# Hybrid stream block on one core: SiLU on ScalarE, two norms from row-major input, decay matrices built together, key products 14 steps later, FFN input sums right after the third norm

## Chip, cores, metric

One Trainium2 chip, one core. The metric is the device time of one launch in microseconds; before the change its median over 3 runs is 1247.88 us (1247.12 to 1248.3).

In this text PE is TensorE, DVE is VectorE, ACT is ScalarE, POOL is GpSimd and SP is SyncE. PSUM is the memory that TensorE writes.

## What is computed

One layer on 512 tokens of width 1024 (float32), batch 1:

```
h  = rmsnorm(x)
qa,ka,va,za,alpha,beta,qb,kb,vb,ga,gb = split(h @ w_in)
q,k,v = silu(causal_conv4(qa,ka,va))
oa = rmsnorm(gated_deltanet(q,k,v,alpha,beta)) * silu(za)      # 8 heads of 128
ob = band attention(qb,kb,vb) with a relative bias               # 16 heads of 64
x  = x + (sigmoid(ga)*(oa@w_a_out) + sigmoid(gb)*(ob@w_b_out)) @ w_o
x  = x + cross attention(rmsnorm(x), rmsnorm(mem))                # 4 heads, 256 memory rows
x  = x + (silu(gate)*up) @ w_down,  gate,up = rmsnorm(x) @ w_gate_up   # 2816 wide
out = rmsnorm(x)
```

In the gated DeltaNet, each head takes, per chunk of 128 tokens here, the matrix `exp(G_i - G_j)` for i >= j (the decay matrix, from cumulated sums G of the log decays), multiplies it into `k k^T` and into `q k^T`, and solves a unit triangular system with the first product.

## The kernel before, in words

Activations lie with features on the 128 partitions and the 512 tokens along the free dimension: x is eight tiles of 128x512. Every product is made in three matmuls from high and low halves (`split`, L113 to L119: ACT makes the high half, DVE or POOL the low half by a subtraction). `weights` (L121) loads a weight block of 128x8x128 (512 KB) on SP's queue and splits it; raw, high and low tiles have three buffers each. A block of eight k steps (`block_steps`, L131) issues three matmuls per step, so 24 per block.

PE's order is the order of the program text; on the other engines and on the DMA queues the framework's scheduler places instructions by a simulated timeline. Side work runs in generators: `drive` (L176) issues one step of the main products and then advances every generator in `pending` by one `yield`; `wait(n)` passes n steps. So the numbers in `wait` set how far behind the main products a dependent PE operation is put. A second generator, `side`, is advanced at a given rate after a given delay.

The stages that matter here, in order:

- **Start.** For k = 0 to 7, x's tile k is loaded, scaled and split, and the products of the first 272 columns (z0: the decay and beta columns and the first two heads' z) are added up in four PSUM banks (L236). `square_sum` (L200) squares each tile on ACT and adds it on POOL (L206). This loop fixes the order of ACT and DVE by hand.
- **First norm** (`first_norm`, L264), beside the z1 products: `rms_cols` (L208) sums the squares over partitions with matmuls against ones and gets the reciprocal root as a column per token tile (the power runs on POOL, L217); `z_evac` (L284) empties the z banks with this scale and makes SiLU from Tanh; `rms_rows` (L220) turns the columns into a row tile `rrow`; POOL multiplies x by it (L276), and the result is split into h. z0, z1 and the keys of heads 0 and 1 use the unscaled x, everything later uses h.
- **Keys.** k0 to k7, with z and gate blocks between them (`go`, L691). `decay` (L306) computes the log decays on small tiles, waits 26 steps, takes the cumulated sums with matmuls (psG, L329), waits 4, transposes them (psT, L334) and writes them to DRAM (dG). `k_after` (L374) does a head's causal convolution (`conv`: one ACT pass, three DVE multiply-adds, Tanh on ACT at L354, one DVE operation at L355), waits 12 steps, multiplies k by itself (kk, L388), takes the norms from its diagonal, loads the head's row of G for all partitions (L399), adds a triangular mask on POOL (L401), exponentiates on ACT (L404), and writes the system's matrix L (L412); after every second head L's 32x32 blocks are stored to DRAM on SP (L423).
- **Values and inverse.** The v blocks (`v_after`, conv and, 12 steps later, the transposes vn at L519), the later gates and z groups, and the first queries. Beside them `inverse_blocks` (L526) gathers L's blocks, inverts them by 31 pairs of DVE operations (L538, L540), and builds up the full inverses with small matmuls from L576 on.
- **Queries, states, outputs, band attention, merge.** `memory` (L835) splits the memory rows' features and computes their norm like the first one.
- **Cross attention**, then **FFN**. The first three of the 22 gate/up column blocks are plain products (`ffn_gemm`, `ffn_after`), during which `ffn_sums` (L1084) builds the normed input in combined halves (fh, fl); the other 19 are done by `unit` (L1136), seven products of half size in place of eight. `gu_split` splits the finished FFN rows for the down projection; for the first five blocks this is done after unit 12.

The norms work with 2 * SiLU(u), that is `(tanh(u/2) + 1) * u`, where later norms divide the factor out; hence the 4s and 0.5 in L393, L416, L482, L519 and thereabouts.

Of the kernel before, what the change touches and what calls it, by code (L numbers as in the profile page):

```python
# [8 lines left out]
F32 = mybir.dt.float32  # L9
F32R = mybir.dt.float32r  # L10
AF = mybir.ActivationFunctionType
ALU = mybir.AluOpType
# [14 lines left out]
NEG = -1e30  # L27

# [11 lines left out]
def hybrid_block(  # L40
    ctx: ExitStack,
    tc: tile.TileContext,
    xT, memT, consts, wz0, wz, wq, wk, wv, wqb, wkb, wvb, wga, wgb,
# [47 lines left out]
    def PD(name):  # L91
# [10 lines left out]
                            pattern=[[1, P]], channel_multiplier=-1)  # L102
    mneg = cp.tile([P, P], F32, name="mneg")
    nc.gpsimd.memset(mneg, 0.0)
    nc.gpsimd.affine_select(out=mneg, in_=mneg, compare_op=ALU.is_ge, fill=NEG, base=0,
# [113 lines left out]

    def rms_rows(rs, ntok, name, dst):  # L220

        ps = PS(name)
        for tt in range(ntok):
            nc.tensor.matmul(out=ps[:, tt * P : (tt + 1) * P], lhsT=rs[:, tt : tt + 1].to_broadcast([P, P]),
                             rhs=ident, start=True, stop=True)
        nc.scalar.activation(dst, ps[:, : ntok * P], AF.Copy)
# [3 lines left out]
    acc1 = TMP("acc", "acc")  # L230
# [13 lines left out]
    with tc.manual_schedule(engines={mybir.EngineType.Activation, mybir.EngineType.DVE}):  # L244
        for k in range(KD):
# [11 lines left out]
            for j in range(max(0, k - 1), k if k < KD - 1 else KD):  # L257
                square_sum(acc1, xt[j], j)
# [5 lines left out]
    def first_norm():  # L264
        yield from wait(1)
        stat["cols"] = rms_cols(acc1, NT, "rstd")
# [7 lines left out]
        for k in range(KD):  # L274
            hi, lo = G("a", "hh", F32R), G("a", "hl", F32R)
            nc.gpsimd.tensor_tensor(out=xt[k], in0=xt[k], in1=rrow, op=ALU.mult)  # L276
            split(hi, lo, xt[k], gain(C_MIX, k))
            h.append((hi, lo))
            yield
# [4 lines left out]
    def z_evac(g):  # L284

        def f(tt, ps):
            o = 16 if g == 0 else 0
            r = stat["cols"][:, tt : tt + 1] if g <= 1 else 1.0
            if g == 0:
                nc.scalar.activation(ab[:, tt, :], ps[:, 0:16], AF.Copy, scale=r)  # L290
            zc, th = TMP("zc", "c")[:, :256], TMP("zt", "th")[:, :256]
            nc.scalar.activation(zc, ps[:, o : o + 256], AF.Copy, scale=r)
            nc.scalar.activation(th, zc, AF.Tanh, scale=0.5)
# [12 lines left out]
    def decay():  # L306
        nc.scalar.activation(beta, ab[:, :, AH:], AF.Exp, scale=-1.0)
        nc.vector.tensor_scalar_add(out=beta, in0=beta, scalar1=1.0)
        nc.vector.reciprocal(out=beta, in_=beta)
        nc.vector.tensor_tensor(out=sp_, in0=ab[:, :, :AH], in1=hrow(C_DT), op=ALU.add)  # L310
        nc.scalar.activation(u_, sp_, AF.Abs)
        nc.scalar.activation(u_, u_, AF.Exp, scale=-1.0)
        nc.vector.tensor_scalar_max(out=sp_, in0=sp_, scalar1=0.0)
        nc.vector.tensor_scalar_add(out=s_, in0=u_, scalar1=2.0)
        nc.vector.reciprocal(out=s_, in_=s_)
        nc.vector.tensor_tensor(out=s_, in0=u_, in1=s_, op=ALU.mult)
        nc.vector.tensor_tensor(out=s2, in0=s_, in1=s_, op=ALU.mult)
        nc.vector.tensor_scalar_mul(out=acc, in0=s2, scalar1=1.0 / 17)
        for i in range(15, 1, -2):
            nc.vector.scalar_tensor_tensor(out=acc, in0=acc, scalar=1.0 / i, in1=s2, op0=ALU.add, op1=ALU.mult)  # L320
        nc.vector.scalar_tensor_tensor(out=acc, in0=acc, scalar=1.0, in1=s_, op0=ALU.add, op1=ALU.mult)
        nc.vector.scalar_tensor_tensor(out=sp_, in0=acc, scalar=2.0, in1=sp_, op0=ALU.mult, op1=ALU.add)
        nc.scalar.activation(ea[:, 0, :], cst[:, C_AL : C_AL + AH], AF.Exp)
        nc.vector.scalar_tensor_tensor(out=g_, in0=sp_, scalar=-1.0,
                                       in1=ea[:, 0:1, :].to_broadcast([P, NT, AH]), op0=ALU.mult, op1=ALU.mult)
        yield from wait(26)
        psG = PS("psG")
        gflat = g_.rearrange("p n h -> p (n h)")
        nc.tensor.matmul(out=psG[:, 0:32], lhsT=tri, rhs=gflat, start=True, stop=True)  # L329
        nc.tensor.matmul(out=psG[:, 32:64], lhsT=ones, rhs=gflat, start=True, stop=True)  # L330
        nc.vector.tensor_copy(Gs, psG[:, 0:32])
        yield from wait(4)
        psT = PS("psT")
        nc.tensor.transpose(out=psT[:32, :P], in_=Gs, identity=ident)  # L334
        nc.scalar.activation(GT, psT[:32, :P], AF.Copy)
        nc.sync.dma_start(out=dG.rearrange("n h c -> (n h) c"), in_=GT)
        nc.scalar.activation(fl(eG), psG[:, 0:32], AF.Exp)
        nc.scalar.activation(fl(eGl), psG[:, 32:64], AF.Exp)
        nc.vector.tensor_scalar_mul(out=fl(negG), in0=psG[:, 0:32], scalar1=-1.0)
        nc.vector.tensor_scalar_mul(out=fl(negeG), in0=fl(eG), scalar1=-1.0)  # L340
        nc.vector.tensor_tensor(out=fl(edec), in0=psG[:, 32:64], in1=fl(negG), op=ALU.add)
        nc.scalar.activation(fl(edec), fl(edec), AF.Exp)


    def conv(ps, ch, dst):

        c = TMP("conv", "c")
        w = lambda i: cst[:, C_CONV + ch * 4 + i : C_CONV + ch * 4 + i + 1]
# [5 lines left out]
        nc.scalar.activation(th, c, AF.Tanh, scale=0.5)  # L354
# [19 lines left out]
    def k_after(hd):  # L374
# [7 lines left out]
        yield from wait(12)  # L382
# [7 lines left out]
        for n in range(NT):  # L390
            c = slice(n * P, (n + 1) * P)
            junk = TMP("junk", "junk", 2, (P, P), pool=ap)
            nc.vector.tensor_tensor_reduce(out=junk, in0=pk[:, c], in1=ident, scale=1.0, scalar=4 * EPS,  # L393
# [3 lines left out]

        pg = TMP("Grow", "ti")
        nc.sync.dma_start(out=chunks(pg), in_=dG[:, hd, :].unsqueeze(0).to_broadcast([P, NT, P]))  # L399
        dec = PT[hd] = TMP("PT", "k0", 2, pool=ap) if hd == 0 else G("b", "PT")  # L400
        nc.gpsimd.tensor_tensor(out=chunks(dec), in0=chunks(pg), in1=mneg.unsqueeze(1).to_broadcast([P, NT, P]), op=ALU.add)  # L401
        for n in range(NT):
            c = slice(n * P, (n + 1) * P)
            nc.scalar.activation(dec[:, c], dec[:, c], AF.Exp, bias=negG[:, n, hd : hd + 1])  # L404
# [11 lines left out]
        nc.vector.scalar_tensor_tensor(out=dinv[hd], in0=sk, scalar=0.5, in1=rk[hd], op0=ALU.mult, op1=ALU.mult)  # L416
# [14 lines left out]
    def q_after(hd):  # L431
# [14 lines left out]
        nc.vector.tensor_scalar(out=fe[hd], in0=sq, scalar1=4 * P * EPS, scalar2=16 * P * EPS * EPS, op0=ALU.mult, op1=ALU.add)  # L446
# [11 lines left out]
    def head_out(hd):  # L458
# [24 lines left out]
        nc.vector.scalar_tensor_tensor(out=f, in0=ss, scalar=4.0 / P, in1=fe[hd], op0=ALU.mult, op1=ALU.add)  # L483
# [28 lines left out]
    def v_after(hd):  # L512
# [3 lines left out]
        yield from wait(12)  # L516
# [173 lines left out]
    gh = lambda j: (gemm(gaps, "ga", wga, j, nc.gpsimd), gate_after(j))  # L690
# [5 lines left out]
    go("v0 v1 g3 v2 v3 g4 v4 v5 g5 z2 v6 v7 g6 z3 q0 q1 g7 q2", side=inverse_blocks(), rate=0.8, delay=22)  # L696
# [138 lines left out]
    def memory():  # L835
        accm = TMP("acc", "acc")[:, :MEM]
        for k in range(KD):
# [8 lines left out]
            square_sum(accm, mk_, k)  # L846
            yield
        yield from wait(4)
        stat["mem"] = rms_cols(accm, 2, "mrs")
        yield from wait(6)  # L850
# [202 lines left out]
    flush()  # L1053
    pending.append(third_norm())

# [284 lines left out]
```

## Time and profile before

| what | us |
|---|---|
| median of 3 runs | 1247.88 |
| the profiled execution | 1245.35 |
| its span | 1243.6 |
| PE busy, of the span | 1203.2 |
| DVE busy | 802.7 |
| ACT busy | 582.7 |
| POOL busy | 192.9 |

Times in the profile are from the span's start. A row of a timeline gives start, length, engine, line, operation, the tile written and those read, the count, and in brackets how long the engine had been idle and what released it. `PEq` or `SPq` is an engine's instruction queue, `PEld` TensorE's weight load. A row of the waits gives the waiting instruction, what released it, and us in total, times, longest. A row of the windows gives the stretch, its length, then each engine's busy us with its count of instructions, and last the granted share of TensorE's clock, the busy share of the DMA engines and GB/s. A group's row has count, busy us, mean ns of one, and the idle time before them; a row by tile or line has shortest/median/longest ns and the first and last start.

### The profile page before, as it was taken

To read this page: it belongs to the slowest core of one execution; us is meant where nothing else is said; L and a number is where in the kernel's file an instruction comes from. 1 tells how busy PE (TensorE), PEld (TensorE's weight loads), DVE (VectorE), ACT (ScalarE), POOL (GpSimd) and SP (SyncE) were. 2 spreads that over 40 slices of the span, in tenths; PEclk is the share of its full clock that TensorE was granted. 3 is DMA by queue.
4 is the path that set the end of the run, shared out by engine and by line. 5 is a ranking of instruction groups with operands and counts; after the bars stand their busy time and mean duration, and the time that the engine had idled before them with its cause. 6 is when DMAs were issued, how large, how long until landed. Compare 5 with 4: busy or idle time off the path is not lost. (4 is left out here: it accounts for less than half of the span.)

```text
span 1243.6 us, 19789 instructions
## 1 busy us (share of the span) xinstructions
PE 1203.2 (97%) x7583; PEld 1049.0 (84%) x7583; DVE 802.7 (65%) x1576; ACT 582.7 (47%) x1203; POOL 192.9 (16%) x172
## 2 busy tenths in 40 slices
PE   7799999999999999999999999999979999999997
PEld 7688787889998887777788898888879999988887
DVE  6988994447553378886365564546878888892234
ACT  5544334355662266665333443434544554562232
POOL 4454122120110000000121300004211111100000
PEclk9999999999999999999999999999989999999998
DMA  6243334211343432322323463113156776743343
GB/s 208 69 148 111 114 123 125 69 60 52 113 130 127 165 111 79 99 77 83 112 85 128 131 208 119 51 35 130 49 144 172 178 174 176 183 124 105 94 118 119
DMA packets 71327, 146.14 MB, mean 118 GB/s; under 512 B 18849, under 2 KB 27457, under 8 KB 71233
## 3 DMA queue, kind: packets, MB, share of 16 engines
q1 hardware_dynamic: 64672, 133.88, 33.9%
q0 software_dynamic: 5472, 9.96, 5.1%
q8 instruction: 59, 0.97, 0.3%
q10 hardware_dynamic: 1088, 1.05, 0.2%
q14 instruction: 36, 0.29, 0.1%
HBM read 136.98 MB, written 7.88 MB: 116 GB/s over the span
## 5 line engine op out<-in xcount | busy, mean ns | idle before, releaser
L114 ACT ACTIVATE whi<-raw 128x1024 fp32r<-128x1024 f32 (+4 forms) x224 | 206.3, 926 | 325.1 <-issue 83.8
L116 DVE TENSOR_TENSOR wlo<-raw,whi 128x1024 fp32r<-128x1024 f32 (+4 forms) x207 | 228.4, 1108 | 139.3 <-ACT whi L114 137.5
L1156 PE MATMUL fp<-fh,whi 128*128 128x256 f32 x532 | 151.5, 285 | 6.3 <-ACT whi L114 6.3
L1158 PE MATMUL fp<-fh,wlo 128*128 128x256 f32 x532 | 152.0, 286 | 3.8 <-DVE wlo L116 3.8
L1157 PE MATMUL fp<-fl,whi 128*128 128x256 f32 x532 | 151.2, 284 | 0.0
L1156 PEld LDWEIGHTS fp<-fh,whi 128*128 128x128 f32 x532 | 102.8, 193 | 7.0 <-ACT whi L114 6.9
L1158 PEld LDWEIGHTS fp<-fh,wlo 128*128 128x128 f32 x532 | 102.7, 193 | 5.3 <-DVE wlo L116 5.3
L1157 PEld LDWEIGHTS fp<-fl,whi 128*128 128x128 f32 x532 | 102.7, 193 | 0.0
L206 POOL TENSOR_TENSOR acc<-acc,sq 128x512 f32<-128x512 f32 (+1 forms) x33 | 47.1, 1427 | 306.7 <-issue 158.2
L114 ACT ACTIVATE whi<-fs 128x512 fp32r<-128x512 f32 x76 | 46.6, 626 | 56.0 <-PE fp L1157 43.4
L116 POOL TENSOR_TENSOR wlo<-raw,whi 128x1024 fp32r<-128x1024 f32 x17 | 41.6, 2445 | 119.9 <-ACT whi L114 108.9
L165 PE MATMUL nat<-whi,hh 128*128 128x256 f32 x192 | 57.2, 298 | 0.0
L116 DVE TENSOR_TENSOR wlo<-fs,whi 128x512 fp32r<-128x512 f32 x76 | 51.3, 686 | 6.8 <-ACT whi L114 6.6
L167 PE MATMUL nat<-wlo,hh 128*128 128x256 f32 x192 | 54.2, 282 | 0.0
L166 PE MATMUL nat<-whi,hl 128*128 128x256 f32 x192 | 54.2, 282 | 0.0
L141 PE MATMUL g<-gul,whi 128*128 128x512 f32 x132 | 51.8, 392 | 1.9 <-DVE gul L116 1.9
L140 PE MATMUL g<-guh,whi 128*128 128x512 f32 x132 | 51.5, 390 | 0.0
L142 PE MATMUL g<-guh,wlo 128*128 128x512 f32 x132 | 51.5, 390 | 0.0
L763 ACT ACTIVATE P<-P,mx 128x128 f32<-128x128 f32 (+1 forms) x64 | 35.8, 560 | 29.6 <-DVE mx L761 29.4
L1143 POOL DMA_DIRECT2D fs<-in_w_u x19 | 16.6, 875 | 150.3 <-DVE wlo L116 50.7
L165 PEld LDWEIGHTS nat<-whi,hh 128*128 128x128 f32 x192 | 36.7, 191 | 0.8
L166 PEld LDWEIGHTS nat<-whi,hl 128*128 128x128 f32 x192 | 36.7, 191 | 0.1
(412 smaller groups left out, 3396.2 us busy)
## 6 DMA issues: line engine op xcount, KB each, us to landing
raw<-in_w_g SPq DMA_DIRECT2D x22, 512.0 KB, 5.5
raw<-in_w_d SPq DMA_DIRECT2D x20, 512.0 KB, 3.5
fs<-in_w_u SPq DMA_DIRECT2D x38, 256.0 KB, 3.8
fs<-in_w_u POOLq DMA_DIRECT2D x19, 256.0 KB, 4.1
fs<-in_w_g POOLq DMA_DIRECT2D x19, 256.0 KB, 6.4
raw<-in_w_u SPq DMA_DIRECT2D x19, 256.0 KB, 4.1
raw<-in_wk SPq DMA_DIRECT2D x8, 512.0 KB, 3.4
raw<-in_wga SPq DMA_DIRECT2D x8, 512.0 KB, 3.3
```

The lines of the kernel that those rows point to most:

```text
L114: nc.scalar.activation(hi, src, AF.Copy, scale=1.0 if scale is None else scale)
L116: (eng or nc.vector).tensor_tensor(out=lo, in0=src, in1=hi.bitcast(F32), op=ALU.subtract)
L140: nc.tensor.matmul(out=ps[:, :w], lhsT=hi[:, k - a, :], rhs=xh[:, n], start=first, stop=False)
L141: nc.tensor.matmul(out=ps[:, :w], lhsT=hi[:, k - a, :], rhs=xl[:, n], start=False, stop=False)
L142: nc.tensor.matmul(out=ps[:, :w], lhsT=lo[:, k - a, :], rhs=xh[:, n], start=False, stop=last)
L165: nc.tensor.matmul(out=o, lhsT=xh[:, tok], rhs=hi[:, kw, :], start=(k == 0), stop=False)
L166: nc.tensor.matmul(out=o, lhsT=xl[:, tok], rhs=hi[:, kw, :], start=False, stop=False)
L167: nc.tensor.matmul(out=o, lhsT=xh[:, tok], rhs=lo[:, kw, :], start=False, stop=(k == KD - 1))
L206: nc.gpsimd.tensor_tensor(out=acc, in0=acc, in1=sq, op=ALU.add)
L1156: nc.tensor.matmul(out=o, lhsT=hi[:, k, :], rhs=xh, start=k == 0, stop=False)
L1157: nc.tensor.matmul(out=o, lhsT=hi[:, k, :], rhs=xl, start=False, stop=False)
L1158: nc.tensor.matmul(out=o, lhsT=lo[:, k, :], rhs=xh, start=False, stop=k == 3)
```

## The change

- `square_sum` no longer serves the first norm and the memory norm. x and mem are also passed row-major (xN, memN); `rms_natural` loads each token tile in two halves on SP, squares them on ACT with the sum along the row as accumulator output, and adds on DVE. It gives the same columns as `rms_cols` without matmuls.
- x times rrow moves from POOL to DVE; so do the FFN's second product with row3 and the low halves of the first three gates' weights.
- SiLU is one ACT pass in z2, z3 and in all convolutions but those of k0 to k2. There, and in z0 and z1, Tanh stays, with the factor 0.5 put into the scale. All now give SiLU, so the constants change.
- `decay` waits 40 steps instead of 26 and is issued at high priority. The decay matrices of all heads are then made in one generator, `decays`: the row goes straight into the matrix tile, a POOL select puts the mask in, and ACT exponentiates. `k_after` waits 26 instead of 12, `v_after` 15 instead of 12. The inverse runs at rate 0.85 after 34 steps instead of 0.8 after 22.
- The memory row is built after 2 more steps instead of 4 + 6.
- `ffn_sums` follows `third_norm` in one chain, where before it was added after the first FFN block. The five early `gu_split`s come one after each of units 9 to 13.

The core of the diff:

```diff
+    def rms_natural(src, ntok, name):
+        ss, rs = SM(name, 2 * ntok), SM(name, ntok, tag=nm(name), bufs=1)
+        for tt in range(ntok):
+            for x in range(2):
+                t = TMP("xn", "ti" if x else "th")
+                nc.sync.dma_start(out=t, in_=src[tt, :, x * T : x * T + T])
+                nc.scalar.activation(t, t, AF.Square, accum_out=ss[:, x * ntok + tt : x * ntok + tt + 1])
+        nc.vector.tensor_tensor(out=rs, in0=ss[:, :ntok], in1=ss[:, ntok:], op=ALU.add)
+        nc.vector.tensor_scalar(out=rs, in0=rs, scalar1=1.0 / D, scalar2=EPS, op0=ALU.mult, op1=ALU.add)
+        nc.gpsimd.tensor_tensor(out=rs, in0=rs, in1=mhalf[:, :ntok], op=ALU.pow)
+        return rs
...
-            for j in range(max(0, k - 1), k if k < KD - 1 else KD):
-                square_sum(acc1, xt[j], j)
...
-        stat["cols"] = rms_cols(acc1, NT, "rstd")
+        stat["cols"] = rms_natural(xN, NT, "rstd")
...
-            nc.gpsimd.tensor_tensor(out=xt[k], in0=xt[k], in1=rrow, op=ALU.mult)
+            nc.vector.tensor_tensor(out=xt[k], in0=xt[k], in1=rrow, op=ALU.mult)
...
+            if g > 1:
+                nc.scalar.activation(zs[g][:, tt, :], ps[:, :256], AF.Silu)
+                return
...
     def decay():
+        with tc.high_priority():
...
-        yield from wait(26)
+        yield from wait(40)
...
+        pending.append(decays())
...
+    def power(hd):
+        for n in range(NT):
+            c = slice(n * P, (n + 1) * P)
+            nc.scalar.activation(PT[hd][:, c], PT[hd][:, c], AF.Exp, bias=negG[:, n, hd : hd + 1])
+    def decays():
+        for hd in range(AH):
+            dec = PT[hd] = TMP("PT", "k0", 2, pool=ap) if hd == 0 else G("b", "PT")
+            nc.sync.dma_start(out=chunks(dec), in_=dG[:, hd, :].unsqueeze(0).to_broadcast([P, NT, P]))
+            nc.gpsimd.affine_select(out=chunks(dec), in_=chunks(dec), compare_op=ALU.is_ge, fill=NEG, base=0,
+                                    pattern=[[0, NT], [1, P]], channel_multiplier=-1)
+            if hd:
+                yield
+                power(hd - 1)
+        power(hd)
+        yield
...
+        if not first:
+            nc.scalar.activation(dst, c, AF.Silu)
+            return
...
-        yield from wait(12)
+        yield from wait(26)
...
-        yield from wait(12)
+        yield from wait(15)
...
-    gh = lambda j: (gemm(gaps, "ga", wga, j, nc.gpsimd), gate_after(j))
+    gh = lambda j: (gemm(gaps, "ga", wga, j, nc.gpsimd if j > 2 else None), gate_after(j))
...
-    go("v0 v1 g3 v2 v3 g4 v4 v5 g5 z2 v6 v7 g6 z3 q0 q1 g7 q2", side=inverse_blocks(), rate=0.8, delay=22)
+    go("v0 v1 g3 v2 v3 g4 v4 v5 g5 z2 v6 v7 g6 z3 q0 q1 g7 q2", side=inverse_blocks(), rate=0.85, delay=34)
...
-        nc.gpsimd.tensor_tensor(out=a, in0=a, in1=row3, op=ALU.mult)
+        nc.vector.tensor_tensor(out=a, in0=a, in1=row3, op=ALU.mult)
...
+    pending.append(seq(third_norm(), ffn_sums()))
     for j in range(NCL):
         drive((ffn_gemm(gps, w_g, j), None), (ffn_gemm(ups, w_u, j), ffn_after(j)))
-        if j == 0:
-            pending.append(ffn_sums())
     flush()
     for j in range(NCL, KF):
         drive((unit(j), None))
-        if j == 12:
-            pending.append(seq(wait(8), gu_splits(range(5))))
+        if 9 <= j < 14:
+            pending.append(seq(wait(8), gu_splits([j - 9])))
```

More of the change, by code (lines that the diff above doesn't have):

```diff
@@ L315, in decay @@
[L315 to L321, printed above, removed]
@@ L330, in decay @@
-        nc.tensor.matmul(out=psG[:, 32:64], lhsT=ones, rhs=gflat, start=True, stop=True)
-        nc.vector.tensor_copy(Gs, psG[:, 0:32])
-        yield from wait(4)
[L333 to L338, printed above, removed]
@@ L396, in k_after @@
                 yield
[L398 to L404, printed above, removed]
+        dec = PT[hd]
         rk[hd], dinv[hd], bD[hd], kds[hd] = s4("rk"), s4("dinv"), s4("bD"), s4("kds")
```

100 lines of the change are left out of this document (59 added, 41 removed).

## Prediction

> **What bounds the kernel now.** I read the page first, then TensorE's waits, then windows around the longest of them, then timelines.
>
> ```profile
> PE 1203.2 (97%) x7583; PEld 1049.0 (84%) x7583; DVE 802.7 (65%) x1576; ACT 582.7 (47%) x1203; POOL 192.9 (16%) x172
> ```
>
> TensorE is busy for 97% of the span. Work taken from DVE, ACT or POOL is worth nothing in itself; only TensorE's waits, its slow clock and its own matmuls can be gained. The waits, summed by who ended them (us, times, longest):
>
> ```profile
> PE fp L1156 <- ACT whi L114: 6.3, 2, 5.0
> PE z L236 <- DVE xgl L118: 4.4, 3, 1.6
> PE fp L1158 <- DVE wlo L116: 3.8, 7, 1.4
> PE psT L334 <- DVE Gs L331: 2.8, 1, 2.8
> PE ka L142 <- DVE wlo L116: 2.6, 1, 2.6
> PE vn L519 <- DVE vT L355: 2.3, 3, 1.1
> ...
> PE kk L388 <- DVE kT L355: 1.3, 1, 1.3
> PE kk L388 <- DVE edec L341: 1.3, 1, 1.3
> ```
>
> Nearly all wait for DVE. Two of them also cost clock, which the windows show (PE, PEld, DVE, ACT, POOL, granted clock):
>
> ```profile
> 59.60:66.40 6.80, 5.52 (x18) 4.45 (x17) 4.27 (x17) 1.94 (x5) 1.54 (x2) 0.50 0.36 102
> 902.70:907.70 5.00, 0.12 (x2) 0.00 (x0) 5.00 (x12) 2.66 (x8) 0.07 (x1) 0.84 0.06 18
> 907.80:912.80 5.00, 3.58 (x15) 3.28 (x16) 2.74 (x7) 0.71 (x2) 1.78 (x2) 0.50 0.82 242
> ```
>
> After the psT wait the clock is 0.50 for 6.8 us, in which 5.5 us of TensorE work would have taken half: 2.8 us lost. After the wait at 902.7 another 3.58 / 2 = 1.8 us are lost. All the waits above and both clock losses come to 29 us; that is the ceiling, apart from matmuls removed.
>
> **The change, part by part.**
>
> *First norm from rows.* Today POOL adds up squares while DVE makes the low halves that TensorE waits for:
>
> ```profile
> 9.95 0.75 DVE L118 SCALAR_TENSOR_TENSOR xgl<-x,cst,xgh 128x512 fp32r<-128x512 f32 x1
> ...
> 19.16 1.75 DVE L118 SCALAR_TENSOR_TENSOR xgl<-x,cst,xgh 128x512 fp32r<-128x512 f32 x1
> ```
> ```profile
> 10.49 11.55 POOL L206 TENSOR_TENSOR acc<-acc,sq 128x512 f32<-128x512 f32 x7 [8.33 <-ACT sq L205]
> 27.63 1.02 POOL L217 TENSOR_TENSOR rstd<-rstd,mhalf 128x4 f32<-128x4 f32 x1 [5.58 <-DVE rstd L215]
> ```
> ```profile
> 24.46 0.67 PE L236 MATMUL z<-wlo,xgh 128*128 128x272 f32 x4
> ...
> 26.40 0.95 PE L212 MATMUL rstd<-ones,acc 128*128 128x1 f32 x8
> ...
> 30.17 1.05 PE L224 MATMUL rrow<-ident,rstd 128*128 128x128 f32 x8
> ```
>
> The same DVE operation takes 0.75 us before POOL starts and 1.75 beside it. The seven POOL additions go, the squares leave the stream that makes the high halves, and the 4.4 us of z waits should go with them. The eight rstd matmul passes (0.95 us, overlapping their neighbours) go too, and four like them in the memory norm: 1.2 us together.
>
> What replaces them: eight more 256 KB loads (2.1 MB), eight ACT squares as now, and one POOL power. SP issues these loads behind x and the two 512 KB loads of z1, and ahead of the key weights.
>
> ```profile
> 9.00:14.00 5.00, 2.09 (x2) 1.00 0.92 358
> ```
>
> This window over L118 (last column GB/s) gives 2.1 MB / 358 GB/s = 5.9 us. L247 issues its last x load at 8.2 us, and these take 5.1 us to land:
>
> ```profile
> L247 SPq DMA_DIRECT2D x<-in_xT x8: 328/432/446, 1.3 to 8.2; - x8
> ```
> ```profile
> DMA to landing us min/median/max: 2.7/5.1/5.5
> ```
>
> So x is in at 13.3, z1's weights 2.9 us later, the rows at about 22.1, and rstd after a square and the 1.02 us power at about 24. With 4.4 us saved, z ends near 20.5, and rrow is reached 30.17 - 24.96 - 0.8 = 4.4 us after that, at about 24.9. That is 1 us of slack on an estimate made of four steps. I charge 0.7 us; the bounds are 0 and 5.9 (rows wholly in the way). The memory norm likewise gets four loads (1 MB, 2.9 us at that rate), and its row is built seven steps sooner; the loads depend on nothing before them, so I take 0, with 2.9 us as the other bound.
>
> *x times rrow moves from POOL to DVE.*
>
> ```profile
> L276 POOL TENSOR_TENSOR x<-x,rrow x8: 1290/1298/1482, 32.3 to 41.6; 128x512 f32<-128x512 f32 x8
> ```
> ```profile
> L317 DVE TENSOR_TENSOR s<-s 128x32 f32<-128x32 f32 x1 | 1.3, 1284 | 0.0
> ```
>
> While POOL does it, a 128x32 DVE operation takes 1.28 us, as long as one POOL instruction: it waits that out. If each of the eight is waited out once, that is up to 10 us of DVE, exchanged for eight operations of at most 0.75 us, 6 us. DVE is some 2 to 4 us ahead and starts earlier with rstd, so I take the whole 2.6 us ka wait as gone; its bounds are 0 and 2.6.
>
> *Decay sums and key products 14 steps later.* A step of TensorE is three matmuls, 43.04 - 42.36 = 0.68 us:
>
> ```profile
> 42.36 0.39 PE L140 MATMUL ka<-xgh,whi 128*128 128x512 f32 x1
> ...
> 43.04 0.39 PE L140 MATMUL ka<-xgh,whi 128*128 128x512 f32 x1
> ```
>
> Fourteen make 9.5 us. psG, psT and kk then stand behind that much more matmul work, against waits of 2.8, 1.3 and 1.3 us. These 5.4 us and the 2.8 us of slow clock should go. kk of head 0 still shares its PSUM buffer with psG, whose last reader is edec, so I keep 0.5 us: 7.7 us gained. With the products move each head's reductions and matrix on DVE, its pow on POOL (now behind the masks), and its stores of L's blocks on SP, which then queue behind more weight loads; only the gather before the inverse reads them (below). Waiting for kk's later place are only the operations of that same head. The low halves of three gates' weights go from POOL to DVE, which the relief of the conv (below) pays for.
>
> [...]
>
> *Decays together.* Eight row loads, eight masks and 32 exponentials now come within some eight steps (5.4 us). On SP the loads stand in one group ahead of weights already requested far in advance. The trace has no mask of 128x512; I bound one by the POOL product above (1.29 us) and by nothing, and take the upper end, since that is the same engine and shape. The exponentials:
>
> ```profile
> L404 ACT ACTIVATE PT<-PT,negG 128x128 f32<-128x128 f32 x32 | 10.0, 390 | 3.8 <-POOL PT L401 3.8
> ```
>
> That is 10 us of ACT in a burst. The high halves of the weights queue behind it. Three weight buffers put them up to two blocks ahead of TensorE, 2 x 8 x 0.68 = 11 us, which covers the burst; without this cover some 5 us of it would show. I take 0.
>
> *SiLU on ACT.* Each conv from the fourth key on, and z2 and z3, loses a DVE operation, while ACT's part stays one pass:
>
> ```profile
> L355 DVE SCALAR_TENSOR_TENSOR vT<-th,conv x8: 684/692/2523, 130.6 to 202.8; 128x512 f32<-128x512 f32 x8
> ```
>
> That shortens the chain to vn by 0.69 us, and its wait grows by three steps, 2.0 us; the longest vn wait is 1.1. All 2.3 us go. Exp and SiLU cost an activation table load at each turn:
>
> ```profile
> 876.25 1.28 ACT L1075 ACT_TABLE_LOAD   x1
> 877.55 0.64 ACT L1075 ACTIVATE fa<-fa 128x512 f32<-128x512 f32 x1
> ```
>
> The next activation starts 1.30 us after the load began, and SiLU takes 0.64 us. I expect two to four more loads, hidden on an engine that is 47% busy. [...]
>
> *The inverse.* Its start moves by 12 steps, key products by 14, the first inverse matmul (at the new rate) by about 7, or 5 us.
>
> ```profile
> L538 DVE TENSOR_TENSOR sub<-Lg,X x31: 191/375/2595, 131.9 to 180.5; 128x31 f32<-128x31 f32 x2, 128x60 f32<-128x60 f32 x2, 128x87 f32<-128x87 f32 x2, 128x112 f32<-128x112 f32 x2
> ```
>
> This DVE chain of 49 us loses about six L355 (4 us), near what the window shrinks. I charge 1.0 us; bounds 0 and 5.
>
> *FFN.* Its sums are emitted five steps sooner, but DVE is already busy 5.00 of 5.00 us before 907.7, so order alone gains little. POOL's product moves to DVE:
>
> ```profile
> L1076 POOL TENSOR_TENSOR fa<-fa,rrow x3: 1507/2882/3632, 878.3 to 899.1; 128x512 f32<-128x512 f32 x3
> ```
> ```profile
> L1092 DVE SCALAR_TENSOR_TENSOR xn<-x,cst,rrow 128x512 f32<-128x512 f32 x8 | 8.0, 1004 | 0.0
> ```
> ```profile
> L116 DVE TENSOR_TENSOR fl<-xn,fh x12: 413/416/1518, 878.5 to 908.3; 128x256 fp32r<-128x256 f32 x12
> ```
>
> Eight xn of 0.75 us would be 6.0, not 8.0, and one fl took 1.1 us too long: 3.1 us of hits go, three operations of 0.69 come: 1.0 us net, taken as 1.5 because the first unit's operands no longer stand behind whole groups of sums. The 5.0 us wait and its slow clock mostly stay; bounds 0 and 6.8.
>
> *gu splits one per unit* instead of five in a row, after which TensorE waited:
>
> ```profile
> 1025.66 0.39 PE L1156 MATMUL fp<-fh,whi 128*128 128x256 f32 x1 [1.34 <-ACT whi L114]
> ```
>
> These 1.3 us and about 0.7 of the small L1158 waits go: 2.0.
>
> **Sum.** 4.4 + 1.2 + 2.6 + 7.7 + 2.3 + 1.5 + 2.0 - 0.7 - 1.0 = 20.0 us. The profiled execution took 1245.35 us (span 1243.6): 1225.4. The runs' median is 1247.88, 2.5 above it, so the median should be 1227.9; I say 1228.
>
> **The rivals.**
> - *Rows too late* (20%). If the 2.1 MB land 5.9 us late, TensorE waits at rrow and the z and ka gains are lost: 20 - 7 = 13, so 1235. For it: four estimated steps, 1 us of slack. Against: 2.9 and 5.9 us are at a measured rate.
> - *FFN wait gone* (12%). If the sums' head start does let the first unit's operands be ready, 6.8 - 1.5 = 5.3 more: 1222.6. Against: DVE's 5.00 of 5.00.
> - *Table loads at every gate* (3%). If Tanh and SiLU need different tables, the later gates between SiLUs bring about 16 loads, 16 x 1.3 = 20.8 us; all on the path, nothing is gained: 1248. Against: ACT's lead of two blocks.
> - *Slower* (5%): the inverse becomes the bound. If everything DVE does from rrow to the inverse is one saturated chain, TensorE's early gains are handed back at the first inverse matmul (L576), and the 14 steps come on top: what is left to gain is 5 us (FFN, gu, the norms' matmuls), the loss 9.5: 1252. It decides once the last key's matrix is later than the gather, so when DVE is over 9.5 - 5 = 4.5 us late there. Against: SiLU relieves DVE.
>
> **How the numbers follow.** The forecast holds 60%. Its own range is 1222 to 1234; to 1238 it takes in a partly late start. Faster by over 0.2% (2.5 us, about what a measurement tells from no change) is 0.92, within it 0.03, slower 0.05.
>
> **What would show it.** L118 at 0.75 us up to 15 us; z ending near 20.5; no rrow wait; clock 1.00 from 50 to 100 us; no psT or vn wait; L1156 waiting still at the first FFN unit. A wait of over 3 us at rrow or at L576 would make it wrong.

## The result, and the profile after

The changed kernel took 1235.5 us, median of four runs (1235.3 to 1237.3), beside 1247.5 for the kernel before in the same rounds: a ratio of 0.990 (95% interval 0.989 to 0.992), so 12.0 us less where 20 had been forecast. The profiled execution took 1235.55 us (span 1233.8, before 1243.6): 9.8 us less. The other 2.2 us of the median are there because the profiled execution of before lay that far below its median, and this one lies on its own. Two executions profiled below, of the kernels with the key products sooner and with Tanh back, and one run with the gu splits in a row were disturbed: from the two profiles only what happens before 195 us is read, and the means below leave all three out.

TensorE's work is nearly what it was, still 97% of the span. DVE's busy time fell by 37 us, POOL's by 49:

```profile
PE 1202.9 (97%) x7571; PEld 1051.2 (85%) x7571; DVE 765.7 (62%) x1564; ACT 585.4 (47%) x1207; POOL 143.5 (12%) x143
```

TensorE's waits, summed as before (us, times, longest):

```profile
PE fp L1188 <- DVE wlo L113: 3.9, 4, 1.9
PE fp L1186 <- ACT whi L111: 3.2, 2, 2.0
PE fp L1187 <- DVE fl L113: 2.0, 1, 2.0
...
PE x L619 <- issue: 1.7, 1, 1.7
...
PE ka L137 <- DVE conv L391: 1.1, 1, 1.1
...
PE nat L162 <- ACT zc L304: 1.0, 1, 1.0
PE ka L137 <- ACT zc L304: 0.9, 1, 0.9
PE nat L164 <- DVE wlo L113: 0.8, 1, 0.8
PE x L619 <- ACT T L615: 0.6, 1, 0.6
PE x L621 <- ACT T L615: 0.5, 1, 0.5
```

The waits at z for DVE, at psT, kk and vn are gone. New are small ones after z, three at the x matmuls of the inverse, and at the first FFN unit three of 2 us or less stand where one of 5.0 stood. The windows show the clock (PE, PEld, DVE, ACT, POOL, granted clock, DMA share, GB/s): full from 50 to 100 us, where before lost 2.8 us, but halved for 6.8 us from 197.1 us on, a place where it had been full:

```profile
50.00:100.00 50.00, 48.89 (x242) 41.00 (x242) 38.46 (x127) 29.91 (x61) 10.08 (x13) 1.00 0.47 146
193.60:197.00 3.40, 1.82 (x71) 1.43 (x59) 0.83 (x2) 1.24 (x4) 0.00 (x0) 1.00 0.37 128
197.10:203.80 6.70, 6.55 (x156) 5.91 (x157) 2.51 (x6) 2.25 (x6) 0.00 (x0) 0.50 0.02 5
```

The way to find where time went is to take the same matmul in both timelines and subtract its start. How much sooner TensorE came to a place, in us:

| first matmul of | before, at | changed | only the row norm undone | only the steps undone | the steps alone, on before |
|---|---|---|---|---|---|
| z1 (nat), after z | 24.96 | 6.4 | 0.2 | 5.8 | 0.7 |
| key block 0 | 38.25 | 3.3 | 0.2 | 3.7 | 0.7 |
| v block 5 | 159.82 | 15.7 | 10.1 | 2.8 | 8.2 |
| v block 7 | 189.44 | 15.8 | 10.2 | 2.9 | 5.0 |
| states (behind the inverse) | 257.78 | 10.8 | 10.4 | 3.4 | 0.2 |
| FFN units | 901.23 | 10.6 | 10.2 | 3.1 | -0.1 |
| last projection | 1199.99 | 9.5 | 5.7 | 0.5 | -2.3 |

The column of the changed kernel says it: 15.8 us were gained by the v blocks, near the forecast, and 5.0 were handed back between v block 7 and the states. (The other columns are experiments, below.) This is that place, first on ACT, then SP's queue, then TensorE:

```profile
184.97 0.76 ACT L615 ACTIVATE T<-t 32x256 f32<-32x256 f32 x2 [0.91 <-PE t L612]
189.66 1.06 ACT L111 ACTIVATE whi<-raw 128x1024 fp32r<-128x1024 f32 x1 [3.92 <-DMA raw<-in_wq]
190.74 0.60 ACT L713 ACTIVATE sga<-ga 128x512 f32<-128x512 f32 x1
191.37 2.34 ACT L615 ACTIVATE T<-t 32x256 f32<-32x256 f32 x6
```
```profile
171.91 0.33 SPq L582 DMA_DIRECT2D d<-X  x1
...
176.07 0.85 SPq L596 DMA_DIRECT2D L<-d  x2
...
184.54 0.91 SPq L120 DMA_DIRECT2D raw<-in_wq  x2
```
```profile
192.18 0.24 PE L619 MATMUL x<-T,L 32*32 32x32 f32 x2 [0.63 <-ACT T L615]
192.97 0.21 PE L621 MATMUL x<-L,T 32*32 32x32 f32 x1 [0.54 <-ACT T L615]
...
197.25 0.25 PE L619 MATMUL x<-T,L 32*32 32x32 f32 x1 [1.68 <-issue]
```

On ACT, six copies of T that TensorE needs start at 191.4 us, behind the high half of a query weight, which waits 3.9 us for its load; SP requested that load at 184.5 us, behind the sixteen gathers. TensorE waits 0.6 and 0.5 us, then 1.7 us for nothing that the profile shows, and the clock is at half for 6.8 us, which by TensorE's 6.55 us of work in it costs an estimated 3.3: 6.1 us. The kernel before had two small waits here:

```profile
PE t L576 <- ACT T L579: 0.6, 1, 0.6
PE x L585 <- issue: 0.5, 1, 0.5
```

Less these 1.1 us it is 5.0, as by position. More than half of the loss is clock.

### The profile page after: what moved, and what is told of

It is laid out like the page before. It is cut to its first block, busy times and chain, and to the rows that moved or that the text cites. A ratio compares the mean times of both kernels' runs of the same rounds, so it can differ in the third digit from the quotient of the medians.

```text
span 1233.8 us, 19731 instructions
## 1 busy us (share of the span) xinstructions
PE 1202.9 (97%) x7571; PEld 1051.2 (85%) x7571; DVE 765.7 (62%) x1564; ACT 585.4 (47%) x1207; POOL 143.5 (12%) x143
## 5 line engine op out<-in xcount | busy, mean ns | idle before, releaser
L203 POOL TENSOR_TENSOR acc<-acc,sq 128x512 f32<-128x512 f32 x19 | 31.1, 1635 | 264.2 <-issue 159.7
L113 POOL TENSOR_TENSOR wlo<-raw,whi 128x1024 fp32r<-128x1024 f32 x14 | 34.0, 2428 | 111.3 <-ACT whi L111 111.3
```

Source lines behind the costliest of these rows:

```text
L113: (eng or nc.vector).tensor_tensor(out=lo, in0=src, in1=hi.bitcast(F32), op=ALU.subtract)
```

## The experiments

Each ran beside the kernel before, in groups of four. The changed kernel itself was run again in the second group, with the steps alone, the two queues and the inverse four steps sooner; its ratio there was 0.994 (0.992 to 0.996) after 0.990. So across groups a run time tells two of these kernels apart only from about 0.4% on (5 us); smaller things are read from the profiles. The loss at the inverse is how much of its lead over before TensorE gives up from v block 7 to the states; DVE's chain is from the start of its first subtraction to that of its copy of the result.

| kernel | ratio to before (95%) | loss at inverse, us | half clock there, us | DVE's chain, us | clock loss / rest, us |
|---|---|---|---|---|---|
| before | 1 | - | 0 | 131.9 to 181.0 | 13.0 / 1233.8 |
| changed, first run | 0.990 (0.989 to 0.992) | 5.0 | 6.8 | 129.5 to 171.9 | 13.3 / 1222.6 |
| changed, again | 0.994 (0.992 to 0.996) | 7.2 | 13.7 | 130.1 to 172.2 | 17.3 / 1222.0 |
| steps undone | 0.999 (0.998 to 1.000) | -0.5 | 0 | 130.8 to 175.7 | 15.1 / 1229.1 |
| steps alone | 1.002 (1.001 to 1.003) | 4.9 | 6.8 | 139.4 to 185.2 | 16.2 / 1232.8 |
| row norm undone | 0.995 (0.993 to 0.996) | -0.2 | 0 | 135.1 to 177.5 | 12.0 / 1226.7 |
| gathers on POOL | 0.995 (0.993 to 0.996) | 5.2 | 10.2 | 129.0 to 171.4 | 13.5 / 1224.8 |
| gathers on two queues | 0.990 (0.988 to 0.992) | 1.7 | 0 | 132.7 to 174.9 | 11.3 / 1222.6 |
| inverse four steps sooner | 0.989 (0.987 to 0.991) | 2.6 | 3.4 | 129.3 to 171.7 | 10.3 / 1222.8 |
| key products sooner | 0.988 (0.987 to 0.990) | - | - | 120.4 to 165.5 | 9.0 / 1221.7 |
| that, and gu splits in a row | 0.988 (0.987 to 0.990) | 0.6 | 0 | 119.0 to 164.0 | 8.6 / 1222.2 |
| Tanh back | 0.994 (0.993 to 0.995) | - | - | 130.2 to 178.3 | 16.5 / 1221.6 |
| FFN as before | 0.995 (0.993 to 0.997) | 5.6 | 13.7 | 128.7 to 171.1 | 16.1 / 1222.8 |
| gu splits in a row | 0.992 (0.990 to 0.994) | 5.9 | 10.2 | 129.0 to 171.5 | 12.8 / 1222.3 |

The last column splits the mean run time. The runs have their mean granted clock on record (those of before beside the changed kernel's first runs excepted); the share that is missing from 1, times the span, is an estimate of the time lost to half clock (it is too high where TensorE waits during half clock), and the rest is what remains. Before has 13.0 and 1233.8 beside the changed kernel's second runs, and a rest of 1233.7 and 1234.1 in the other two groups. So the change takes 11 to 12 us out of the rest. The kernels with the row norm and without the old step counts, the two with sooner key products among them, stay within 1221.6 and 1222.8, but for the gathers on POOL; what tells them apart in run time is how much half clock they meet, from 8.6 to 17.3 us.

**The steps, undone and alone.** In the changed kernel, the steps to the decay's sums, the key products and vn, and the inverse's start:

```diff
-        yield from wait(40)
+        yield from wait(26)
-        yield from wait(26)
+        yield from wait(12)
-        yield from wait(15)
+        yield from wait(12)
-side=inverse_blocks(), rate=0.85, delay=34)
+side=inverse_blocks(), rate=0.8, delay=22)
```

> The changed kernel with the old step counts: the decay's sums after 26 steps, key products after 12, vn after 12, the inverse at delay 22 and rate 0.8. Theory A (the 14 steps are what took away the waits at psT and kk and the half clock there, and 3 steps the vn waits): waits of 2 to 5 us and the half clock of 2.8 us come back between 50 and 100 us, part of the inverse's loss goes, and the time is 4 to 9 us longer, 1240 to 1244. Rival B (SiLU on ACT and the lighter DVE alone took them away, the steps only moved the inverse): the time is 1230 to 1235, the inverse's 5 us back.

And the reverse edit, alone, in the kernel before:

> The kernel before with the step counts of the change alone: 40 steps to the decay's sums, 26 to the key products, 15 to vn, inverse at delay 34 and rate 0.85. Nothing else is changed. Theory A (the steps are what takes the psT, kk and vn waits and the half clock away, 5.4 + 2.8 + 2.3 us, and the inverse gives up to 3 back): about 1238 to 1240 where before is 1247.5. Rival D (the steps pay only with the DVE work that SiLU and the row norm take away; without it the products' reductions come in the way of later convs, and the gather before the inverse is late): 1245 to 1252.

Undone, nearly all is lost (0.999): 7 us in the rest. TensorE's waits from 40 to 165 us, with the steps undone:

```profile
PE psG L343 <- DVE g L337: 6.5, 1, 6.5
PE kk L431 <- DVE kT L398: 1.8, 1, 1.8
PE vn L555 <- ACT vT L394: 1.7, 1, 1.7
PE kk L431 <- ACT kT L394: 0.7, 1, 0.7
```

TensorE comes to the sums sooner than before and simply waits there longer, and 6.8 us of half clock follow from 51.6 us on: theory A, and a little more than it said. Alone, the steps gain 8.2 us by v block 5. Of these 3.1 go before v block 7, where TensorE waits 2.4 us for a conv on DVE and the clock is halved for 3.4 us, and 4.9 at the inverse, whose gather is late, as rival D says:

```profile
139.38 0.19 DVE L538 TENSOR_TENSOR sub<-Lg,X 128x31 f32<-128x31 f32 x1 [2.23 <-DMA Lg<-d]
```

The gather lands at 139.3 us, 7.5 later than in the kernel before. This is the "slower" rival of the prediction, on the steps alone. The last key product starts 3.5 us later than in the kernel before (125.0 after 121.5), and from there to the gather are 14.4 us instead of 10.4. In the whole change the last key product starts at 117.7 and the gather lands 11.8 us behind it; without the row norm it is 123.3, and 11.8 again. So most of what pulls the gather back is that TensorE comes there sooner, 5.6 us of it by the row norm; the shorter way behind the key products gives 2.6.

**The row norm undone.** `rms_natural(xN, NT, "rstd")` becomes the sum of squares and `rms_cols(acc1, NT, "rstd")` of before.

> The changed kernel with the first norm's sums as before: squares of the eight x tiles on ACT, added on POOL, summed by eight small matmuls; no loads of rows. All else as changed. Theory A (the row loads save 6.4 us of z waits and give 3.1 back, because the second half of z1's weights lands behind them and rstd comes late): z waits of 4 us and more return, the waits at nat and rrow after it go, net 3.3 us slower, about 1239. Rival B (the 3.1 us come from the copies of the z groups standing in ACT's queue behind the high halves of h, whatever makes rstd): 6.4 us slower, 1242. Rival C (the swap is worth nothing, what DVE gains is lost at rrow): 1235.5.

The z waits are back (4.4 us in three, for xgl), and no wait stands between z and key block 0: the row norm gives 6.2 us and takes 3.1 back, as theory A and the table say. The median, 1238.8, is what A named, but not by A's way: in the profile TensorE reaches the states 10.4 us sooner than before, as with the row norm (10.8). The 5.6 us that the norm gains by v block 7 are lost again at the inverse, and the other difference to the changed kernel arises in the FFN units, which this edit does not touch. By the rest of the run time the norm is worth 4 to 5 us.

This kernel also shows that a late chain does not settle the loss. TensorE and the chain are both 5.6 us later than in the changed kernel, so the first query weights are requested as far behind the start of v block 7, 10.9 us in both. Yet nothing is lost here: the high half starts 4.3 us after the request instead of 5.1, ACT waits 3.1 us for it instead of 3.9, TensorE waits once, 0.4 us, for T, and the clock stays full:

```profile
194.43 1.06 ACT L111 ACTIVATE whi<-raw 128x1024 fp32r<-128x1024 f32 x1 [3.10 <-DMA raw<-in_wq]
```
```profile
185.00:220.00 35.00, 34.42 (x628) 30.00 (x626) 11.38 (x18) 14.89 (x30) 2.40 (x1) 1.00 0.36 95
```

**The inverse.** Three edits and then a fourth. First all sixteen gathers from SP to POOL (`nc.sync.dma_start` to `nc.gpsimd.dma_start` at L595 and L596):

> The changed kernel with one edit: the sixteen gathers of the inverse's blocks (L595, L596) are issued from POOL's queue instead of SP's; the order of the instructions on TensorE, ACT and DVE is the same. Theory A (five us were given back around the inverse because the query weights are requested only at 184.5 us, behind those gathers, and ACT's queue stands behind that load with the copies that the inverse's matmuls need): the load is requested about 8 us sooner, ACT's wait of 3.9 us ahead of that whi is gone, the half clock at 197 us does not come, and the time is 5 us less, about 1230.5 us, ratio to before 0.986. Rival B (the inverse's own chain of copies and small matmuls costs that much whenever it runs, and the clock drops with it): 1235.5, ratio 0.990.

The first query weights were requested at 174.1 instead of 184.5, and ACT no longer waited for them. Yet the loss stayed: POOL's gathers landed at 189.4, 3.1 us later than SP's, and TensorE now waited for them, twice, with the clock at half:

```profile
PE t L612 <- DMA X<-d: 1.5, 2, 0.9
```
```profile
187.20:197.40 10.20, 10.20 (x159) 8.79 (x161) 2.64 (x2) 4.07 (x9) 5.39 (x2) 0.50 0.52 190
```

So theory A's forecast failed; but as the edit put one wait in place of another, it shows only that ACT's wait is not the one way to be late. Then the eight gathers into L from ACT's queue (L596 alone to `nc.scalar.dma_start`), and the inverse four steps sooner with four steps more behind the gathers (`delay=30`, `wait(24)`):

> The changed kernel with one edit: the eight gathers into L (L596) are issued from ACT's queue, the eight into X stay on SP, behind the query weights instead of ahead of them; the order of TensorE's and DVE's work is the same. Theory A (TensorE loses 5 us at the inverse because the query weights, and with them the copies of T behind them on ACT, are a microsecond too late, and sparse work then brings the half clock): the load is requested at about 176 us instead of 184.5, the gathers land no later, no half clock near 197 us, the first state matmul 16 us before that of the kernel before instead of 10.8, and 5 us less in all, 1230. Rival B (that work brings the half clock whenever TensorE comes there this early; in the run with POOL's queue it came with two waits of 0.9 us): 1235.

> The changed kernel with the inverse's start four steps sooner (delay 30 instead of 34) and four steps more between its gathers and its first matmuls (24 instead of 20), so that TensorE's part of it stands where it stood. Theory A (as for the gathers on two queues): gathers and query weights are requested 2 to 3 us sooner, ACT's wait for them is shorter by as much, TensorE's waits of 0.6, 0.5 and 1.7 us and the half clock at 197 us go, 1230.5. Rival C (the chain of subtractions on DVE is what sets the gathers' time, and cannot start sooner): gathers where they were, 1235.5.

With two queues there was no half clock at the inverse and only 1.7 us were lost, but from a smaller lead: 3.4 us of half clock at 85.7 us had come before, TensorE was at v block 7 only 12.8 us sooner than before, and at the states 11.1, hardly more than the changed kernel's 10.8. The time, 1233.3, lies between A's and B's. ACT's first gather held everything behind it: ACT ended an operation at 172.65 us, issued its eight gathers from 178.95 us on, and started its next operation only at 185.8. By ACT's waits:

```profile
ACT conv L389 <- DMA L<-d: 13.2, 1, 13.2
```

Starting the inverse sooner moved nothing on DVE: the chain ended at 171.7, the query weights were requested at 184.5, as before. That is rival C. It still lost less, in one wait of 2.5 us and 3.4 us of half clock, and beside the changed kernel it ran at 0.989 against 0.994. So DVE's chain sets when gathers and query weights come, but not alone what is lost. To move the chain, what is before it has to move: the steps to the key products fewer from head to head, more steps between the gathers and the first matmuls, and the inverse's start sooner:

```diff
-        yield from wait(26)
+        yield from wait(26 - 2 * hd)
-        yield from wait(20)
+        yield from wait(30)
-side=inverse_blocks(), rate=0.85, delay=34)
+side=inverse_blocks(), rate=0.85, delay=22)
```

> The changed kernel with the key products of the later heads sooner: 26 - 2 x head steps instead of 26 for all (12 for the last), the inverse started at delay 22 instead of 34, and 30 steps instead of 20 between its gathers and its first matmuls, which stay where they were. Theory A, as it stands now (what limits the inverse is one chain that begins with the last key products: stores of L, its gather landing at 129.0 us, 43 us of DVE work at over 90% busy to 171.9, then stores, gathers, and behind these on SP the query weights; TensorE came 16 us sooner, the gather only 2.9): the gather lands 6 to 9 us sooner, the query weights 5 to 8 us sooner, no wait at x and no half clock near 197 us, and the first state matmul 15 to 16 us before that of the kernel before instead of 8.4 to 10.8: 1229 to 1231 where the changed kernel's first look was 1235.5. Rival B (DVE is as full before 129 us as behind it, the chain ends no sooner): no change.

> The same as the one before (key products of later heads sooner, inverse sooner, 30 steps between), and the five gu splits in a row after unit 12 as in the kernel before. If the splits one per unit do cost 1 to 2 us at the units of 1004 to 1040 us (the profiles show TensorE losing 0.3 to 2.0 us between the tenth and the thirteenth mark there in six kernels with them and gaining 1.1 in the one without), this is 1 to 2 us faster than the one before, 1228; otherwise the same.

DVE in the changed kernel, its chain's first and last operations:

```profile
129.50 0.18 DVE L574 TENSOR_TENSOR sub<-Lg,X 128x31 f32<-128x31 f32 x1
...
171.91 1.12 DVE L579 COPY Lg<-X 128x1024 f32<-128x1024 f32 x1
```

The same, and SP, in the kernel with both edits:

```profile
119.01 0.19 DVE L574 TENSOR_TENSOR sub<-Lg,X 128x31 f32<-128x31 f32 x1 [1.66 <-DMA Lg<-d]
...
163.99 1.12 DVE L579 COPY Lg<-X 128x1024 f32<-128x1024 f32 x1
```
```profile
169.99 0.32 SPq L595 DMA_DIRECT2D X<-d  x1
...
178.91 0.85 SPq L120 DMA_DIRECT2D raw<-in_wq  x2
```

The chain starts 10.5 us sooner and ends 7.9 sooner, the query weights are requested 5.6 us sooner, T is waited for nowhere, and the clock stays full:

```profile
190.00:220.00 30.00, 28.20 (x519) 24.95 (x519) 8.50 (x15) 11.30 (x24) 2.40 (x1) 1.00 0.14 46
```

1.8 us of waits for nothing shown stay. The last key product starts 10.2 us sooner, about as much as the chain. The states start 14.0 us sooner than before. Both kernels with this edit ran at 0.988, 1231.5 and 1230.7 us. That is faster than the kernel before by 1.2%, and than the changed one by 0.2% (against its first runs, where the intervals overlap) to 0.6% (against its second). Against the inverse four steps sooner, 0.989, no difference shows. By the last column of the table the whole gain on the changed kernel is clock, 8.6 or 9.0 us lost instead of 13.3 and 17.3; the rest is the same. So moving the chain goes with less half clock, and neither it nor the few steps has been shown to be the only remedy.

**SiLU undone.** All convs and z2, z3 by Tanh with halved weights and a product on DVE (`first` always true):

> The changed kernel with SiLU back as Tanh on ACT and one product on DVE, in all convs and in z2 and z3 (weights halved beforehand, so no further scaling); the rest as changed. Theory A (SiLU's main worth is that it shortens the chain on DVE between the gather and the stores of the inverse, 49 us before and 43 after): the chain ends 4 to 6 us later, vn waits of up to 2 us return, and the time is 5 to 7 us longer than the changed kernel on the same chip. Rival E (three more steps before vn are enough, and DVE has room for six more operations of 0.69 us): no vn waits, the same time within 1.5 us, and two table loads fewer on ACT.

The chain took 48.1 us instead of 42.4 and ended 6.4 later, so TensorE waited 3.1 us for the gathers' data; that much of A is shown. But no vn wait returned, and none is left with the steps alone, so the three steps are enough for those (E). The run time, 0.994, lies within what the changed kernel itself showed, and its rest, 1221.6, is no longer than the changed kernel's. SiLU's worth, if there is any, is then in the clock; how much stays open.

**The FFN.** As before: sums after the first pair of blocks, the product with row3 on POOL.

> The changed kernel with the FFN as before: third norm before the first gate block, input sums only after the first pair of blocks, and the product with row3 on POOL. Theory A (moving them gained nothing that shows: the first unit's operands come late in both, the wait of 5.0 us and its half clock before, waits of 2.0, 2.0 and 1.5 us and a half clock after): TensorE loses at the first unit within 1 us of what the changed kernel loses there, whole time the same within 1.5 us. Rival F (the forecast's 1.5 us are there and are lost in the later units by other causes): the first unit alone 1.5 us or more later.

At the first unit this kernel lost 0.6 us of its lead, the changed one 0.4, and the rests are 1222.8 and 1222.0: theory A. Of before's 5.0 us wait the changed kernel has this:

```profile
894.60 0.39 PE L1187 MATMUL fp<-fl,whi 128*128 128x256 f32 x1 [2.03 <-DVE fl L113]
897.09 0.58 PE L1186 MATMUL fp<-fh,whi 128*128 128x256 f32 x1 [1.99 <-ACT whi L111]
899.09 0.58 PE L1188 MATMUL fp<-fh,wlo 128*128 128x256 f32 x1 [1.21 <-DVE wlo L113]
```

**The gu splits** in a row after unit 12, as before, and the changed kernel again for reference:

> The changed kernel with one edit: the five gu splits after unit 12 in a row, as before, instead of one after each of units 9 to 13. Theory A (the splits between a unit's own splits push TensorE's operands late, a wait of 1.3, one of 2.1 and a half clock of 3.4 us near 1004 us): these waits go, the wait of 1.3 us after the five comes back, and the time is about 2 us less, 1233.5. Rival B (the waits there come from the late landing of an accumulating load that has nothing to do with the splits): the waits stay, 1235.5 to 1237.

> The changed kernel itself, beside the other three on one chip: 1235.5 us, ratio to before 0.990. Its first look and that of the run with the gu splits in a row differ by under 1 us in every stage up to the FFN and by more in the FFN units. If the waits near 1004 us and the half clock there are a matter of when accumulating loads land in that one execution, they will stand at other units here, and differ by 1 to 4 us; if the splits cause them, they stand at the same units.

The changed kernel waits in unit 13:

```profile
1003.97 0.39 PE L1186 MATMUL fp<-fh,whi 128*128 128x256 f32 x1 [1.18 <-ACT whi L111]
1006.37 0.58 PE L1188 MATMUL fp<-fh,wlo 128*128 128x256 f32 x1 [1.91 <-DVE wlo L113]
```

From the start of unit 13 to that of unit 16 the changed kernel lost 1.6 us of its lead in the first profile and 1.8 in the second, each with 3.4 us of half clock there (from 1006.0 and 1012.1 us), which before had not; with the splits in a row two kernels gained 1.1 and 0.1, the first without half clock. But one kernel with single splits gained 2.0 there (gathers on POOL), and in run time the row is worth nothing that shows (0.988 and 0.988; 0.992 beside 0.990 and 0.994). This stays open. What is settled is that the 2.0 us forecast did not come.

## Why the prediction was right in direction, with 8 us too much gain

The time is that of the rival of late rows, 1235, and its way is not: no wait for rstd stands at rrow. It lies above the forecast's own range, 1222 to 1234, and inside the wider one, to 1238, which was given for a partly late start; the time is there for other reasons, so that this range held it is luck. In the profile 9.8 of the 20.0 us came. Of the 10.2 missing, 4.0 are at the inverse, 3.6 at the gu splits, 1.9 at the FFN's first unit and 1.2 ahead of key block 0, with small differences of either sign elsewhere. Outside the clock the sum had 20.0 - 2.8 = 17.2 us, and the estimate above has 11 to 12. By the prediction's own steps, measured on the profiled execution:

- **z and rstd, 4.4 + 0.8 of the 1.2: right in the cause, low in size.** L118's operation, now L115, takes 0.75 us in all eight places; z ends at 18.5, 6.4 sooner, and 5.2 to 6.2 sooner in the ten other profiles with the row norm.

```profile
L115 DVE SCALAR_TENSOR_TENSOR xgl<-x,cst,xgh x8: 742/746/752, 5.9 to 14.3; 128x512 fp32r<-128x512 f32 x8
```

- **Norm late, -0.7: mis-sized, -3.1, within its bounds.** (The 0.8 of rstd's matmuls are in this -3.1.) The last row tile's square started at 22.1 us, where the rows had been forecast, and rrow came at 24.4 without a wait for rstd, but with less than 0.1 us of slack, not 1. What was overlooked is what else queues in this stretch: z1's second half on SP behind row loads, and the z copies on ACT (L304).

```profile
20.38 0.39 PE L162 MATMUL nat<-whi,xgh 128*128 128x256 f32 x1 [0.24 <-ACT whi L111]
21.64 0.39 PE L164 MATMUL nat<-wlo,xgh 128*128 128x256 f32 x1 [0.76 <-DVE wlo L113]
30.89 0.39 PE L162 MATMUL nat<-whi,xgh 128*128 128x256 f32 x1 [1.00 <-ACT zc L304]
34.95 0.50 PE L137 MATMUL ka<-xgh,whi 128*128 128x512 f32 x1 [0.93 <-ACT zc L304]
```

- **ka, 2.6: right** (2.8 from key block 0 to 2). **psT, kk, clock, vn, 7.7 + 2.3: right** (9.6 from key block 2 to v block 5, against 10.0); a new wait of 1.1 for a conv is in it. The masks cost 0.64 us each, half the bound taken.

```profile
L370 POOL TENSOR_SCALAR_AFFINE_SELECT PT<-PT x8: 634/636/644, 67.3 to 76.9; 128x512 f32<-128x512 f32 x8
```

- **Tables: right in number** (six loads of 1.28 us, two before: four more). They start at 0.8, 62.5, 65.9, 84.1, 429.8 and 867.4 us; none stands between 84.1 and 429.8, where the gates' Tanh (to 239.1 us) and SiLU take turns, so that rival is out.
- **The inverse, -1.0: this is the term that failed most**, -5.0 and -7.2 in two profiles, at and over its bound of 5. That "this DVE chain of 49 us loses about six L355 (4 us), near what the window shrinks" was right in kind (it lost 6.7, 49.1 to 42.4 us), but the window was measured from the wrong end. The chain starts when the last key products are stored. With 14 more steps in front these started 3.8 us sooner than before, while TensorE came to the v blocks up to 16 us sooner, so the chain's start moved by 2.4 us only. Charging the first inverse matmul 5 us hid that TensorE had moved so much more than the chain. And that 6.8 us of half clock would follow waits of 0.6, 0.5 and 1.7 us at the small matmuls, 6 us lost in place of 3, was not in the sum at all. Waits of that size were not always followed by it: with both edits the clock stayed full behind those of 1.2 and 0.6 us.
- **FFN 1.5: -0.4**, just below its lower bound of 0 (-1.1 to 0.1 in the other profiles with this FFN). DVE is relieved as forecast (L1122 0.75 us each), but the first unit still waits for its operands, at three places instead of one, and the half clock stays. **gu splits 2.0: -1.6** in the profile, with 3.4 us of half clock near 1006 us in it, cause open.

The half clock at psT did go with the wait: 6.8 us of it before, none from 50 to 100 us now, so the sum, which took the 2.8 us of clock together with the wait, was right there. In the changed kernel TensorE was busy for 1.82 us of the 3.4 us before the clock fell at 197 us.

## What to carry to other kernels

Where TensorE is the bound and is made faster, ask of each long side chain not how long it is but what event starts it, and whether that event moved as much as TensorE did; if it moved less, the gain can come back further on as waits, and in slow clock: here 2.8 us of waits at the inverse, and 6.8 us of half clock behind them. Delaying the work that such a chain begins with, to clear an early wait, should be graded: the items that the chain gets last are delayed least. A part of a change tested alone can look worthless because a later stage absorbs it (the steps: 8.2 us gained and none left), so read positions along the trace and not the total. And where kernels differ by less than a per cent, take the granted clock of each run out of its time before saying which of them does less waiting: here 13.3 and 17.3 us of clock loss in the same kernel looked like 0.990 and 0.994.

## What the runs showed of the hardware

The half clock at the inverse lasted 3.4, 6.8, 10.2 or 13.7 us in different profiles: one, two, three and four times the 3.41 us that the half clock at 1006.02 us lasts in the changed kernel. The changed kernel itself had 6.8 in one profile and 13.7 in another, and 10.2 with only later work changed:

```profile
196.30:209.90 13.60, 13.17 (x193) 11.86 (x194) 3.19 (x7) 3.23 (x8) 0.00 (x0) 0.50 0.01 2
```

The moments can be read from the traces of the changed kernel and of the one before. In the changed kernel the clock falls to half at 197.06, 896.79, 1006.02 and 1227.88 us, so 699.73, 109.23 and 221.86 us apart: 205, 32 and 65 times 3.4133. In the kernel before it falls at 59.57, 906.08 and 1237.17 us, 846.51 and 331.09 us apart: 248 and 97 times 3.4133. Whether such moments are why like lags cost 5.0 us in one profile and nothing in another was not shown: no run moved them alone. The time is less certain too: the changed kernel's second runs lie between 1236.1 and 1246.8 us, the nineteen of before beside them between 1243.7 and 1249.6.

The pause of 1.7 us at the x matmuls, for which the profile names no releaser, stands directly behind a dense run of 32x32 matmuls. Such pauses, of 0.9 to 2.1 us, are in eight of the thirteen profiles beside that of before, whose longest is 0.5. Whether TensorE waits for instructions there was not tried.
